# Softmax reciprocals and gates multiplied into the probabilities, and a new entry into each attention stage

## The chip, the cores and the metric

The kernel runs on one core of a Trainium2 chip. The metric is the device time of one execution in microseconds (us), the median of several executions. The engines are named as the profile names them: PE (TensorE matmuls) and PEld (its weight loads), DVE (VectorE), ACT (ScalarE), POOL (GpSimd) and SP (SyncE, which here only issues loads).

## What is computed

Two layers over 256 tokens of 1024 features. Each layer normalises its input, projects it (one weight matrix), runs a dilated attention of 24 heads and a sparse attention of 8 query heads over 2 key heads with three gated branches, merges both, and adds a convolutional FFN. The part that the change touches is the division by the softmax sums:

```
def dilated_mixer(q, k, v):                       # three groups of 8 heads
    for gi, (window, dil) in enumerate(DIL_PAIRS):
        o, lse = banded_attention(...)            # softmax(q k^T / 8) v, and its log-sum
    wts = softmax(stack(lses), axis=0)
    o = sum(wts * stack(outs))
...
    p2 = softmax(s2);  o_sel = p2 @ vg            # selected blocks
    o_win = banded_attention(q, k_win, v_win)     # window
    g = sigmoid(gate_logits)
    o = g[0] * o_cmp + g[1] * o_sel + g[2] * o_win
```

In the dilated attention the three groups of a head share one softmax denominator, so that the result is a sum of unnormalised products divided once.

## The kernel before

**Weights.** All projections stream through `units` of 128 x 2048 fp32, in an order fixed in advance. `load_half` (L208) loads half a unit (512 KB) on SP into one of five `raw` buffers. Each half is split on the chip: ACT casts it to fp32r (`hi`, L238), DVE subtracts (`lo`, L239). A product then takes three matmuls: hi with the activations' high half (L290), hi with their low half (L291), lo with the high half (L292).

**Stages of a layer.** `c10` and `c11` (2 units each: keys and values of the sparse branch, the compressed branch's input), `bq` (its queries), nine chunks of the dilated heads with four `merge` units between, four more merges, two projections, `out`, then the FFN: 22 up units and the down units. The norm's factor 1/rms is worked out beside the first stage: squares are summed into `fin`, summed over partitions by matmuls on `ones` (L344), raised to -1/2 on POOL (L347), copied into the diagonals `dg` (L351), and applied when PSUM is read (L419).

**Attention work.** It is written as generators that run between the weights' matmuls: `tick()`, called after each half chunk, runs one split, the rotary chains (`rope_run`), and one step of up to five active jobs. `job_a(hp)`, four per layer, does two heads' dilated attention, `job_b(hp, t)`, eight per layer, the selected and the window branch of two heads for one block of 128 queries. Both write scores to `pt` (SBUF), take exponentials there with the sums as a by-product, transpose the probabilities on PE (`transposed`, L576), and multiply by the values (`col_pair`, L571). The result lies feature by token, so its division needs the reciprocals along the free axis: DVE copies them, 64 times each, into `drb` (L673, L759), `spread` transposes that with two matmuls (L595), ACT copies the result to `sc` (L597), and DVE multiplies (L706, L772); job_b then adds its two branches (L773).

**Tables and the compressed branch.** POOL multiplies the rotary tables with the gains (`tabs`, L394; `tabc`, L397) once `gr` has landed (L387). `job_cmp1` copies keys (`cdup`, L792), transposes them (L795) and writes them in residue order with copies of a quarter each on ACT (L802).

**Order on the engines.** The scheduler of the tile framework reorders each engine's instructions after that; each engine then runs its list in order, and a wait holds all behind it.

## Time and profile before

| | |
|---|---|
| three timed runs | 965.47, 968.27, 968.22 us |
| median | 968.22 us |
| the profiled execution's own time | 964.59 us |
| its span (first to last instruction) | 962.8 us |
| PE busy | 936.6 us (97%) |
| DVE busy | 753.0 us (78%) |
| ACT busy | 580.2 us (60%) |
| POOL busy | 154.7 us (16%) |
| DMA | 172 GB/s, 165.95 MB |

Busy shares are averages over stages that differ: PE's 97% says that it sets the time nearly everywhere, not that the others have room everywhere. The views of the trace that go further are the list of waits (how long an engine stood idle, and for what), the timeline of a stretch, and busy times by window. In a row, the bracket at the end gives the idle time of the engine ahead of the instruction and what ended it. The granted clock is full in all forty slices of the page.

### The profile page before, as it was taken

The numbers are of one execution on the slowest core, as the hardware profiler recorded it, in microseconds if no ns is written. First come the engines' busy times: TensorE is split into PE (matmuls) and PEld (weight loads), VectorE is DVE, ScalarE is ACT, GpSimd is POOL, SyncE is SP. The second block draws the span as 40 slices with busy tenths as digits, with TensorE's granted clock in tenths as the row PEclk, the third lists the DMA queues.
The fourth block names the chain that finished last, engine by engine and source line by source line (L and its number), as shares of the span: only waits on it lengthen the run. The fifth ranks groups of instructions, "written<-read, shape, count | busy, mean of one in ns | idle before, by whom it ended". The sixth has DMA issues, their size and how long they took to land.

```text
span 962.8 us, 18575 instructions
## 1 busy us (share of the span) xinstructions
PE 936.6 (97%) x7122; PEld 848.9 (88%) x7122; DVE 753.0 (78%) x1595; ACT 580.2 (60%) x1186; POOL 154.7 (16%) x179
## 2 busy tenths in 40 slices
PE   6899999999999999999998999999999999999998
PEld 4778887878999999999986787877799999999998
DVE  6898866887679889986478987678876888998742
ACT  6778665666556555555456986466755555655431
POOL 6140211212002111110122301122200111111000
PEclk9999999999999999999999999999999999999999
DMA  7734446525456565666455344554354465666660
GB/s 242 255 132 155 150 157 207 189 88 174 148 162 213 180 210 187 189 196 204 147 168 174 112 151 135 196 196 140 121 180 153 161 217 175 205 197 203 196 209 19
DMA packets 48041, 165.95 MB, mean 172 GB/s; under 512 B 6096, under 2 KB 7632, under 8 KB 47824
## 3 DMA queue, kind: packets, MB, share of 16 engines
q1 hardware_dynamic: 46800, 163.71, 52.1%
q8 instruction: 56, 0.92, 0.4%
q10 hardware_dynamic: 1152, 1.05, 0.3%
q14 instruction: 33, 0.27, 0.1%
HBM read 163.69 MB, written 1.05 MB: 171 GB/s over the span
## 4 chain that ended last, share of the span: by engine, by line
PE 78%; DVE 10%; ACT 6%; issue 2%; POOL 1%; DMA 1%; SPq 0%; DVEq 0%; ACTq 0%; POOLq 0%
PE acc L373 25%; PE acc L290 5%; PE acc L292 5%; PE acc L291 5%; DVE lo L239 4%; PE acc L1082 4%; PE acc L1084 4%; PE acc L1083 4%; PE acc L957 3%; PE att L571 3%; PE acc L959 3%; PE acc L958 3%; PE att L576 2%; PE acc L993 2%; PE acc L994 2%
## 5 line engine op out<-in xcount | busy, mean ns | idle before, releaser
L239 DVE TENSOR_TENSOR lo<-raw,hi 128x1024 fp32r<-128x1024 f32 (+1 forms) x292 | 368.4, 1279 | 51.6 <-ACT hi L238 49.4
L238 ACT CAST hi<-raw 128x1024 fp32r<-128x1024 f32 (+1 forms) x292 | 294.0, 1037 | 150.9 <-PE acc L291 36.9
L373 PE MATMUL acc<-u,hi 128*128 128x256 f32 x1376 | 236.3, 277 | 0.0
L373 PEld LDWEIGHTS acc<-u,hi 128*128 128x128 f32 x1376 | 207.4, 188 | 0.1
L373 PE MATMUL acc<-u,lo 128*128 128x256 f32 x688 | 190.2, 276 | 0.0
L290 PE MATMUL acc<-hi,hT 128*128 128x512 f32 (+1 forms) x384 | 154.0, 401 | 8.7 <-ACT hi L238 8.7
L292 PE MATMUL acc<-lo,hT 128*128 128x512 f32 (+1 forms) x384 | 150.0, 391 | 5.2 <-DVE lo L239 5.1
L291 PE MATMUL acc<-hi,hT 128*128 128x512 f32 (+1 forms) x384 | 148.5, 387 | 0.0
L373 PEld LDWEIGHTS acc<-u,lo 128*128 128x128 f32 x688 | 129.1, 188 | 0.0
L1084 PE MATMUL acc<-act,lo 128*128 128x256 f32 x352 | 97.2, 276 | 0.0
L1082 PE MATMUL acc<-act,hi 128*128 128x256 f32 x352 | 97.2, 276 | 0.0
L1083 PE MATMUL acc<-act,hi 128*128 128x256 f32 x352 | 97.2, 276 | 0.0
L290 PEld LDWEIGHTS acc<-hi,hT 128*128 128x128 f32 x384 | 72.6, 189 | 25.9 <-ACT hi L238 11.1
L292 PEld LDWEIGHTS acc<-lo,hT 128*128 128x128 f32 x384 | 72.4, 189 | 23.6 <-DVE lo L239 9.2
L291 PEld LDWEIGHTS acc<-hi,hT 128*128 128x128 f32 x384 | 72.7, 189 | 12.6 <-issue 0.3
L957 PE MATMUL acc<-hT,hi 128*128 128x256 f32 x256 | 73.4, 287 | 0.0
L959 PE MATMUL acc<-hT,lo 128*128 128x256 f32 x256 | 71.8, 281 | 0.0
L958 PE MATMUL acc<-hT,hi 128*128 128x256 f32 x256 | 71.7, 280 | 0.0
L1084 PEld LDWEIGHTS acc<-act,lo 128*128 128x128 f32 x352 | 66.1, 188 | 0.0
L1082 PEld LDWEIGHTS acc<-act,hi 128*128 128x128 f32 x352 | 66.1, 188 | 0.0
L1083 PEld LDWEIGHTS acc<-act,hi 128*128 128x128 f32 x352 | 66.1, 188 | 0.0
L1054 POOL TENSOR_TENSOR z<-z,rb 128x512 f32<-128x512 f32 x22 | 30.5, 1386 | 203.1 <-DVE z L1053 203.1
(215 smaller groups left out, 1690.2 us busy)
## 6 DMA issues: line engine op xcount, KB each, us to landing
raw<-in_ws_dram SPq DMA_DIRECT2D x300, 512.0 KB, 4.6
raw<-in_ws_dram SPq DMA_DIRECT2D x8, 280.0 KB, 4.2
x<-in_x_dram SPq DMA_DIRECT2D x1, 1024.0 KB, 9.6
out_dram<-x ACTq DMA_DIRECT2D x8, 128.0 KB, 2.7
gr<-in_g_rope_dram SPq DMA_DIRECT2D x2, 384.0 KB, 4.4
masks<-in_mask_dram SPq DMA_DIRECT2D x1, 576.0 KB, 7.6
xo<-in_xo_dram SPq DMA_DIRECT2D x2, 256.0 KB, 4.5
xo<-in_xo_dram SPq DMA_DIRECT2D x1, 512.0 KB, 7.0
```

Source lines behind the costliest of these rows:

```text
L238: A.copy(h, r)
L239: V.tensor_sub(l, r, h.bitcast(F32))
L290: T.matmul(o, a_hi, b_hi, start=first, stop=False)
L291: T.matmul(o, a_lo, b_hi, start=False, stop=False)
L292: T.matmul(o, a_hi, b_lo, start=False, stop=last)
L373: return [lambda a=a: T.matmul(a[0], a[1], a[2], start=a[3], stop=a[4]) for a in todo]
L957: T.matmul(o, hi[:, k, ms], hT[:, 0, k], start=k == 0, stop=False)
L958: T.matmul(o, hi[:, k, ms], hT[:, 1, k], start=False, stop=False)
L959: T.matmul(o, lo[:, k, ms], hT[:, 0, k], start=False, stop=k == 7)
L1082: T.matmul(ps, hi[:, c], act[:, 0, k], start=k == 0, stop=False)
L1083: T.matmul(ps, hi[:, c], act[:, 1, k], start=False, stop=False)
L1084: T.matmul(ps, lo[:, c], act[:, 0, k], start=False, stop=k == NFT - 1)
```

## The change

It has four parts.

1. **Probabilities scaled.** `job_a` and `job_b` multiply the reciprocals (in `job_b` also the gates) into `pt` by a product per column block, ahead of the transposes; `spread`, `drb`, `sc` and the product on the result go. `job_b`'s two branches accumulate in one PSUM region and leave it with one copy. In `job_a` the reciprocals are four columns per head instead of two, and the yields stand elsewhere; `job_b` normalises the first head one tick after its softmax, and starts with one yield more.
2. **Start.** The first activations and the gain are loaded from ACT's queue, the first unit in quarters on SP; 14 matmuls on `ones` precede the first product; the feeds alternate with the casts; squares are taken in pairs on ACT and added on DVE, none on POOL; c10's first half runs k outside, token block inside.
3. **Entry of each layer.** c10's evictions wait until all of c10 is multiplied; c11 fetches both units and runs token block by token block; `job_cmp1` starts after c11, and its transposes multiply by a permutation, so that the copies `T` are contiguous; the tables are built in three pieces; `dg` is on ACT; the copy `rd` comes a step earlier; `qS` is allocated earlier.
4. **FFN norm.** The norm's matmuls move from before the last weight slice of the first unit to after the third matmul of the second.

```diff
-    A.activation(warm, warm, AF.Square)
+    idle = att()
+    for i in range(14):
+        T.matmul(idle[:, 0:P], ones, ones, start=True, stop=True)
...
+            step = w // 4 if (i, w // 4) in early else w // 2
+            for c0 in range(0, w, step):
...
+        if src is not x:
+            if m % 2:
+                sq = com.tile([P, 2, S], F32, name="sq2", bufs=2)
+                A.activation(sq, src[:, m - 1:m + 1], AF.Square)
+                if m > 1:
+                    V.tensor_add(sq, sq, sums["acc"])
+                sums["acc"] = sq
...
         for t in range(2):
-            V.tensor_scalar(dg[:, t * P:(t + 1) * P], ident, r[:, 1, t:t + 1], None, op0=ALU.mult)
+            A.activation(dg[:, t * P:(t + 1) * P], ident, AF.Copy, scale=r[:, 1, t:t + 1])
...
+            if c == "c11":
+                unit(0)
+                for t in range(2):
+                    for kh in range(2):
+                        if t == 0 and kh == 1:
+                            unit(1)
+                        mms(kh, t, range(4), kh == 0, kh == 1)
+                        if kh == 1:
+                            post_fn(t, ps[t])
+                        tick()
+                return
...
-                        if c == "c10" and t == 0:
+                    if kh == 1 and (c != "c10" or t == 1):
+                        if c == "c10":
                             nrm["col"] = rstd_col()
+                            post_fn(0, ps[0])
                         post_fn(t, ps[t])
...
-        def spread(drb):
-            ps = att()
-            for i in range(2):
-                T.transpose(ps[:, i * P:(i + 1) * P], drb[:, i].rearrange("p a d -> p (a d)"), ident)
-            sc = pool.tile([P, S], F32, name="sc", bufs=1)
-            A.copy(sc, ps[:, 0:S])
-            return sc
...
-            drb = pool.tile([P, 2, 2, 64], F32, name="drb", bufs=1)
-            V.tensor_copy(drb, dr.rearrange("p a t -> p t a")[:, :, :, None].to_broadcast([P, 2, 2, 64]))
+            for a in range(2):
+                for w, (o, n) in enumerate(((0, P), (P, S), (384, S), (640, S))):
+                    V.tensor_scalar(pts[a][:, o:o + n], pts[a][:, o:o + n], dr[:, a, w:w + 1], None, op0=ALU.mult)
+            yield
             yield from take("pT", 2)
             e = [transposed(pts[a], 0, 4) for a in range(2)]
             yield
-            sc = spread(drb)
...
-            V.tensor_tensor(res, o[:, 0:S], sc, op=ALU.mult)
-            split_evac(oT["a"][:, 0, hp], oT["a"][:, 1, hp], res)
+            split_evac(oT["a"][:, 0, hp], oT["a"][:, 1, hp], o[:, 0:S])
...
+            def normalize(a, pt):
+                V.reciprocal(d[:, 1, :, a], d[:, 0, :, a])
+                V.tensor_tensor(d[:, 1, :, a], d[:, 1, :, a], gs[:, t, 1:3, 2 * hp + a], op=ALU.mult)
+                for b in range(2):
+                    V.tensor_scalar(pt[:, b * nk:(b + 1) * nk], pt[:, b * nk:(b + 1) * nk], d[:, 1, b, a:a + 1], None,
+                                    op0=ALU.mult)
...
-            V.tensor_tensor(ob, o[:, 0:S], sc, op=ALU.mult)
-            V.tensor_add(ob_all()[:, hp, tok], ob[:, 0:P], ob[:, P:S])
+            V.tensor_copy(ob_all()[:, hp, tok], o[:, 0:P])
...
-                pg = unit({42: rstd_col}, True)
-                pu = unit({24: lambda: box.update(rb=rstd_row()), 30: lambda: post_g(0, pg)})
+                pg = unit({}, True)
+                pu = unit({3: rstd_col, 27: lambda: box.update(rb=rstd_row()), 33: lambda: post_g(0, pg)})
...
+        A.dma_start(xo[:, 0:2], xv[:, 0:2])
+        A.dma_start(gain, g_norm.rearrange("p (a k) -> p a k", k=8))
+        A.dma_start(xo[:, 2:4], xv[:, 2:4])
...
         for m in range(8):
-            if m in (1, 3):
-                if m == 1:
-                    prepare(0)
+            feed(hT, m, 0, False, xo)
+            if m < 4:
                 pend.popleft()[1]()
-            feed(hT, m, 0, False, xo)
```

How the instructions stand, before and now. Line numbers of the changed kernel are some 4 to 50 higher: L243 is the subtraction `lo`, L242 the cast `hi`, L625 the transposes of the probabilities, L620 the products with the values, L1006 to L1008 a merge's matmuls (before L957 to L959).

PE, layer 0, where the first two products of job_b stand in a merge, before:

```order
L292 MATMUL acc<-lo,hT 128x512
L595 MATMUL att<-ident,drb 128x128 x2
L571 MATMUL att<-pT,vB 64x128 x4
L957 MATMUL acc<-hT,hi 128x256
L958 MATMUL acc<-hT,hi 128x256
L959 MATMUL acc<-hT,lo 128x256
L595 MATMUL att<-ident,drb 128x128 x2
L571 MATMUL att<-pT,vB 64x128 x8
L957 MATMUL acc<-hT,hi 128x256
L576 MATMUL att<-ident,pt 128x128 x2
L958 MATMUL acc<-hT,hi 128x256
```

and the same work now:

```order
L1007 MATMUL acc<-hT,hi 128x256
L625 MATMUL att<-ident,pt 128x128 x4
L1008 MATMUL acc<-hT,lo 128x256
L1006 MATMUL acc<-hT,hi 128x256
L625 MATMUL att<-ident,pt 128x128
L1007 MATMUL acc<-hT,hi 128x256
L625 MATMUL att<-ident,pt 128x128
L1008 MATMUL acc<-hT,lo 128x256
```

and a little later:

```order
L1008 MATMUL acc<-hT,lo 128x256
L1006 MATMUL acc<-hT,hi 128x256
L620 MATMUL att<-pT,vB 64x128 x12
L625 MATMUL att<-ident,pt 128x128 x6
L1007 MATMUL acc<-hT,hi 128x256
```

The two transposes on `drb` ahead of each product are gone, and the transposes of `pt` stand in smaller groups between the merge's matmuls. Over the whole program PE goes from one kind of matmul to another (weights, transposes, attention products) 280 times before and 270 times now, and the transposes by identity or permutation fall from 410 to 362; with the spreads taken out of the order before and all else as it was, the changes of kind would be 252.

DVE, layer 0, behind the reciprocals of job_a for the second head pair, before:

```order
L673 COPY drb<-dr 128x256
L848 TENSOR_TENSOR gl<-gl 128x128
L437 TENSOR_TENSOR t_2111<-qraw,tabs 128x128
L849 TENSOR_SCALAR gl<-gl 128x128
L427 TENSOR_REDUCE rss<-t_2055 128x2
L850 TENSOR_TENSOR gl<-gl 128x128
L377 TENSOR_SCALAR rss<-rss 128x2
L427 TENSOR_REDUCE rss<-t_2059 128x6
L436 TENSOR_TENSOR t_2055<-qraw,tabs 128x128
L377 TENSOR_SCALAR rss<-rss 128x6
L440 TENSOR_TENSOR t_2055<-t_2055,t_2111 128x128
L239 TENSOR_TENSOR lo<-raw,hi 128x1024
```

and now:

```order
L716 TENSOR_SCALAR pt<-pt,dr 128x256
L243 TENSOR_TENSOR lo<-raw,hi 128x1024
L894 SCALAR_TENSOR_TENSOR gl<-gl 128x128
L457 TENSOR_TENSOR t_2045<-t_2045,t_2101 128x128
L896 TENSOR_SCALAR hr<-gl 128x512
L716 TENSOR_SCALAR pt<-pt,dr 128x256 x2
L716 TENSOR_SCALAR pt<-pt,dr 128x128
L716 TENSOR_SCALAR pt<-pt,dr 128x256 x3
L243 TENSOR_TENSOR lo<-raw,hi 128x1024
```

Two of the eight products (one stands seven rows higher) come ahead of the subtraction `lo`, the other six between it and its second half; before, one copy stood there.

ACT at the kernel's start, before:

```order
L310 ACTIVATE hT<-xo,gain 128x256 x2
L238 CAST hi<-raw 128x1024
L310 ACTIVATE hT<-xo,gain 128x256
L325 ACTIVATE sq<-xo 128x256
L310 ACTIVATE hT<-xo,gain 128x256
L325 ACTIVATE sq<-xo 128x256
L310 ACTIVATE hT<-xo,gain 128x256
L325 ACTIVATE sq<-xo 128x256
L310 ACTIVATE hT<-xo,gain 128x256
L325 ACTIVATE sq<-xo 128x256
L238 CAST hi<-raw 128x1024 x2
```

and now:

```order
L314 ACTIVATE hT<-xo,gain 128x256
L242 CAST hi<-raw 128x512
L314 ACTIVATE hT<-xo,gain 128x256
L326 ACTIVATE sq_125<-xo 128x512
L242 CAST hi<-raw 128x512
L314 ACTIVATE hT<-xo,gain 128x256
L242 CAST hi<-raw 128x512
L314 ACTIVATE hT<-xo,gain 128x256
L326 ACTIVATE sq_135<-xo 128x512
L242 CAST hi<-raw 128x512
L314 ACTIVATE hT<-xo,gain 128x256 x2
L326 ACTIVATE sq_144<-xo 128x512
```

Casts of a quarter alternate with the feeds, and squares are taken two slices at a time.

POOL from layer 0's first memset of the job tables on, before:

```order
L784 MEMSET pad 128x16
L806 MEMSET F 128x32 x2
L347 TENSOR_TENSOR rstd<-rstd,mhalf 128x2
L394 TENSOR_TENSOR tabs<-cossin,gr 128x640 x2
L397 TENSOR_TENSOR tabc<-ropec,gr 128x128
```

and now:

```order
L826 MEMSET pad 128x16
L847 MEMSET F 128x32 x2
L411 TENSOR_TENSOR tabs<-cossin,gr 128x2x128 x2
L411 TENSOR_TENSOR tabs<-cossin,gr 128x2x64 x2
L411 TENSOR_TENSOR tabs<-cossin,gr 128x2x128 x2
L359 TENSOR_TENSOR rstd<-rstd,mhalf 128x2
L980 TENSOR_TENSOR tabc<-ropec,gr 128x128
L390 TENSOR_TENSOR rss<-rss,mhalf 128x2 x4
```

All pieces of the tables come ahead of the norm's power; before, the power came first. On SP, `gr` stood ahead of the masks and of three halves of c11, and stands behind them now.

## Rows read from the trace of the kernel before

**Rows 1.** The page, part 1: busy time, share of the span, instructions of each engine
```profile
PE 936.6 (97%) x7122; PEld 848.9 (88%) x7122; DVE 753.0 (78%) x1595; ACT 580.2 (60%) x1186; POOL 154.7 (16%) x179
```

**Rows 2.** Waits of PE, whole span: us in total, times, longest
```profile
PE acc L290 <- ACT hi L238: 8.7, 4, 7.1
PE acc L292 <- DVE lo L239: 5.1, 8, 2.2
```

**Rows 3.** Timeline, first 23 us, ACT and PE: start, us, instruction [idle before <-releaser]
```profile
5.99 1.04 ACT L238 CAST hi<-raw 128x1024 fp32r<-128x1024 f32 x1 [0.67 <-DMA raw<-in_ws_dram]
7.08 0.80 PE L290 MATMUL acc<-hi,hT 128*128 128x512 f32 x1 [7.08 <-ACT hi L238]
15.27 2.54 ACT L238 CAST hi<-raw 128x1024 fp32r<-128x1024 f32 x3
16.35 0.50 PE L290 MATMUL acc<-hi,hT 128*128 128x512 f32 x1 [0.76 <-ACT hi L238]
22.41 0.29 PE L290 MATMUL acc<-hi,hT 128*128 128x280 f32 x1
```

**Rows 4.** Timeline, POOL and DVE around the mixing norms and the first FFN norm
```profile
19.95 3.11 POOL L394 TENSOR_TENSOR tabs<-cossin,gr 128x640 f32<-128x640 f32 x2
21.46 2.10 DVE L351 TENSOR_SCALAR dg<-ident,rstd 128x128 f32<-128x128 f32 x2
310.79 0.48 DVE L351 TENSOR_SCALAR dg<-ident,rstd 128x128 f32<-128x128 f32 x2
489.03 3.42 DVE L337 TENSOR_TENSOR fin<-acc,sq 128x128 f32<-128x128 f32 x2
```

**Rows 5.** Timeline, PE, stalls after c10: layer 0 first and last, layer 1 likewise
```profile
25.77 0.40 PE L292 MATMUL acc<-lo,hT 128*128 128x280 f32 x1 [2.18 <-DVE lo L239]
49.78 0.44 PE L485 MATMUL att<-ident,rd 128*128 128x128 f32 x2 [0.78 <-DVE rd L482]
499.50 0.66 PE L795 MATMUL att<-ident,cdup 128*128 128x128 f32 x4 [1.52 <-DVE cdup L792]
514.89 0.44 PE L485 MATMUL att<-ident,rd 128*128 128x128 f32 x2 [1.81 <-DVE rd L482]
```

**Rows 6.** Timeline, DVE and PE at layer 0's FFN norm
```profile
307.88 0.48 DVE L311 SCALAR_TENSOR_TENSOR u<-x,gain,u 128x256 fp32r<-128x256 f32 x1
308.75 0.61 PE L344 MATMUL att<-ones,fin 128*128 128x1 f32 x4 [1.55 <-DVE fin L333]
```

**Rows 7.** Timeline, PE, one spread in its place
```profile
76.07 0.39 PE L291 MATMUL acc<-hi,hT 128*128 128x512 f32 x1
76.30 0.39 PE L292 MATMUL acc<-lo,hT 128*128 128x512 f32 x1
76.53 0.38 PE L595 MATMUL att<-ident,drb 128*128 128x128 f32 x2
76.84 0.66 PE L571 MATMUL att<-pT,vB 128*64 128x128 f32 x8
```

**Rows 8.** Single lines, DVE: ns min/median/max, first and last start, forms
```profile
L673 DVE COPY drb<-dr x8: 286/290/294, 126.7 to 732.8; 128x256 f32<-128x256 f32 x8
L759 DVE COPY drb<-db x16: 276/287/295, 73.5 to 594.9; 128x256 f32<-128x256 f32 x16
L706 DVE TENSOR_TENSOR res<-att,sc x8: 411/420/424, 142.9 to 743.7; 128x256 f32<-128x256 f32 x8
L849 DVE TENSOR_SCALAR gl<-gl x2: 217/218/220, 174.1 to 648.7; 128x128 f32<-128x128 f32 x2
L855 DVE TENSOR_SCALAR hr<-gl x2: 412/414/415, 178.1 to 652.7; 128x512 f32<-128x512 f32 x2
```

**Rows 9.** Windows: us, busy PE, PEld, DVE, ACT, POOL (instructions), PEclk, DMA, GB/s
```profile
50.00:75.00 25.00, 25.00 (x127) 19.76 (x125) 24.31 (x76) 19.42 (x54) 9.07 (x9) 1.00 0.40 133
530.00:565.00 35.00, 34.87 (x222) 28.31 (x220) 33.50 (x124) 31.65 (x93) 8.47 (x10) 1.00 0.39 130
```

**Rows 10.** Timeline, PE, behind job_a of layer 0's second head pair
```profile
176.92 0.50 PE L292 MATMUL acc<-lo,hT 128*128 128x512 f32 x1 [0.36 <-DVE lo L239]
```

More of the change, by code (lines that the diff above doesn't have):

```diff
@@ L233, in prepare @@
                 else:
-                    raw = load_half(i, c0, w // 2)
-                c = slice(c0, c0 + w // 2)
+                    raw = load_half(i, c0, step)
+                c = slice(c0, c0 + step)
                 def halve(h=hi[:, c], l=lo[:, c], r=raw):
@@ L318, in feed @@
                 V.scalar_tensor_tensor(lo, v, gc, hi.bitcast(F32), op0=ALU.mult, op1=ALU.subtract)
+        if src is not x:
[5 more added lines that the diff above has]
+                sums["acc"] = sq
+            if m == 7:
+                sums["fin"] = com.tile([P, S], F32, name="fin", bufs=1)
+                V.tensor_add(sums["fin"], sq[:, 0], sq[:, 1])
+            return
         if m == 0:
@@ L420, in attention_layer, with rope_run @@
         ready = {"b": 0, "o": 0, "t": 0, 0: 0, 1: 0, 2: 0, 3: 0}
-        def rope_run(raw, kind, t, nh, ksc, fin):
+        def rope_run(raw, kind, t, nh, ksc, fin, pre=None):
             t1 = pool.tile([P, 8, 64], F32, name="t1", bufs=4)[:, :nh]
@@ L489, in fin @@
                 ready["b"] += 1
-            start(rope_run(kraw[:, t, b].rearrange("p (h d) -> p h d", d=64), 3 + b, t, 2, None, fin))
+            start(rope_run(kraw[:, t, b].rearrange("p (h d) -> p h d", d=64), 3 + b, t, 2, None, fin, pre))
         def post_bq(t, ps):
@@ L606, in job_a @@
             ds = pool.tile([P, 2, 4], F32, name="ds", bufs=2)
-            dr = pool.tile([P, 2, 2], F32, name="dr", bufs=2)
+            dr = pool.tile([P, 2, 4], F32, name="dr", bufs=2)
             rows = [slice(0, 64), slice(64, P)]
@@ L750, in job_b @@
             yield
+            normalize(0, p0)
+            p1 = softmax(1, s1)
+            yield
             yield from take("pT", 2)
             e.append(transposed(p0, 0, 2 * (t + 1)))
-            p1 = softmax(1, s1)
+            normalize(1, p1)
             yield
-            yield
-            V.reciprocal(d[:, 1], d[:, 0])
-            V.tensor_tensor(d[:, 1], d[:, 1], gs[:, t, 1:3, 2 * hp:2 * hp + 2], op=ALU.mult)
-            drb = pool.tile([P, 2, 2, 64], F32, name="drb", bufs=1)
-            V.tensor_copy(drb, d[:, 1, :, :, None].to_broadcast([P, 2, 2, 64]))
             e.append(transposed(p1, 0, 2 * (t + 1)))
@@ L762, in job_b @@
             yield
-            sc = spread(drb)
             o = att()
-            for b in range(2):
-                col_pair(o, [(lambda z, b=b: z[:, b * P:(b + 1) * P],
-                              lambda h, b=b, kt=kt: vB[:, kt, b, kv * 64:(kv + 1) * 64],
-                              [e[h][:, b * (t + 1) + kt] for h in range(2)]) for kt in range(t + 1)], True, True)
+            col_pair(o, [(lambda z: z[:, 0:P], lambda h, b=b, kt=kt: vB[:, kt, b, kv * 64:(kv + 1) * 64],
+                          [e[h][:, b * (t + 1) + kt] for h in range(2)]) for b in range(2) for kt in range(t + 1)], True, True)
             give("pT", 2)
             yield
-            ob = pool.tile([P, S], F32, name="res", bufs=1)
-            V.tensor_tensor(ob, o[:, 0:S], sc, op=ALU.mult)
-            V.tensor_add(ob_all()[:, hp, tok], ob[:, 0:P], ob[:, P:S])
+            V.tensor_copy(ob_all()[:, hp, tok], o[:, 0:P])
             ready["o"] += 1
@@ L932, in job_cmp2, with job_tables @@
                 ready["t"] += 1
+        def job_tables():
+            table(2, 3)
+            yield
+            table(0, 2)
+            yield
+            G.tensor_tensor(tabc, ropec, gr[:, :, 5, :], op=ALU.mult)
         chunk_in("c10", 512, post_c10)
+        side.append(job_tables())
+        chunk_in("c11", 280, post_c11)
         side.append(job_cmp1())
-        chunk_in("c11", 280, post_c11)
         nrm["row"] = rstd_row()
@@ L1095, in block_kernel, with quarters @@
         xv = xo_in.rearrange("p (k q) -> p k q", k=8)
-        nc.sync.dma_start(xo[:, 0:2], xv[:, 0:2])
-        nc.sync.dma_start(gain, g_norm.rearrange("p (a k) -> p a k", k=8))
-        early[0, 0] = load_half(0, 0, UW // 2)
+        def quarters(i, h):
+            raw = com.tile([P, UW // 2], F32, name="raw", bufs=5)
+            for j in range(2):
+                c = slice(j * 512, (j + 1) * 512)
+                early[i, h * 1024 + j * 512] = raw[:, c]
+                nc.sync.dma_start(raw[:, c], ws[i][:, h * 1024 + j * 512:h * 1024 + (j + 1) * 512])
+        A.dma_start(xo[:, 0:2], xv[:, 0:2])
+        A.dma_start(gain, g_norm.rearrange("p (a k) -> p a k", k=8))
+        A.dma_start(xo[:, 2:4], xv[:, 2:4])
+        A.activation(warm, warm, AF.Square)
+        quarters(0, 0)
         mhalf = com.tile([P, 16], F32, name="mhalf")
         G.memset(mhalf, -0.5)
-        nc.sync.dma_start(xo[:, 2:4], xv[:, 2:4])
-        early[0, UW // 2] = load_half(0, UW // 2, UW // 2)
+        quarters(0, 1)
         nc.sync.dma_start(xo[:, 4:8], xv[:, 4:8])
```

80 lines of the change are left out of this document (48 added, 32 removed).

## The prediction

> **What bounds the kernel now.** I read the page first: TensorE (PE) is busy 936.6 of 962.8 us [rows 1], so the end is set by how many matmuls there are, at what pace, and by the few places where PE stands still. The view of waits says which these are: the largest two, 8.7 us on ScalarE's (ACT) casts `hi` and 5.1 us on VectorE's (DVE) subtractions `lo`, are waits for a weight half that isn't split yet [rows 2]. The timeline then shows where: nearly all of it lies in the first 17 us [rows 3], where both layers enter their attention stage [rows 5], and at the FFN's norm [rows 6]. Between these PE runs at its pace, 0.23 us from one 128x512 matmul to the next [rows 7]. What the change can win is therefore entry stalls and matmuls taken out; what it can lose is time where DVE, which it loads more, has no slack. DVE is the engine to look at: 24.31 of 25 us busy in 50 to 75 us, and 33.50 of 35 in the same stretch of layer 1 [rows 9].
>
> **The change, part by part.**
>
> *1. Kernel start.* Before, ACT casts the first 512 KB half at 5.99 us and PE starts at 7.08; ACT then works through all eight feeds and their squares before it casts the second unit at 15.27, so PE waits until 16.35, and the first 48 matmuls (c10) end at 22.41 [rows 3]: 15.33 us for what takes 48 x 0.23 = 11.0 at the pace of [rows 7]. Now the first half comes in quarters, from a queue that carries no `xo`, the first cast is half as long, and no square stands on GpSimd (POOL), whose sums ACT's squares waited for. The first cast, at about half of 1.04 us and behind one feed, can end near 6.2 instead of 7.03; the second unit's cast, no longer behind the chain of POOL sums, near 13.2 instead of 16.3. Then 24 matmuls (5.5 us) and about a microsecond for a late `lo` give an end of c10 near 19.9: gain 2.5 us. The 14 idle matmuls on `ones` run while PE would wait for data; if they hang over, they cost at most 0.8 us, and I put them at nothing because the first cast covers them.
>
> *2. Rest of layer 0's entry.* Five more stalls between 22.4 and 50 us add up to 4.46 us: 2.18, 0.37, 0.40, 0.73 and 0.78 (the first and the last of them in [rows 5]). The first is a `lo` that came late because DVE was held: the two `dg` products took 2.10 us together while POOL ran the tables, and 0.48 at the FFN's norm where POOL was idle [rows 4]. Now `dg` is on ACT, `cdup`'s transposes stand inside bq with work ahead of them, c11's units are fetched in one go, and the copies `T` are two instead of eight per head pair, which frees ACT for casts. I leave 1.5 us of the 4.46: gain 3.0. Parts 1 and 2 together 5.5; bounds 2.5 (only the start) and 8 (no stall left).
>
> *3. Layer 1's entry.* Four stalls, 1.52, 0.41, 0.72 and 1.81, again 4.46 us (the first and the last of them in [rows 5]). Same cures; the last is a chain for `rd`, whose copy now comes a step earlier. I leave 1.2: gain 3.3, bounds 1.5 and 4.5.
>
> *4. FFN norm.* PE waits 1.55 us for `fin` at 308.75, and once more in layer 1. Moving the norm's matmuls into the second unit doesn't give that back: the matmuls that are now first need `u`'s low half, which DVE ends at 307.88 + 0.48 = 308.36, only 0.39 earlier [rows 6]. Gain 2 x 0.35 = 0.7, bounds 0 and 1.4.
>
> *5. No spread.* Each of 24 spreads is two transposes that take 0.31 us up to the next matmul [rows 7]; 0.22 of it are the transposes and about 0.09 is the change from one kind of matmul to another, which stays, since the fp32 product follows anyway. 20 x 0.21, and 4 at 0.37 that stood between two groups of fp32 products and go whole: 5.7 us, bounds 4.8 and 7.4 (with every switch). It comes straight off the bound engine. ACT's 24 copies `sc` go too, off the path.
>
> *6. Transposes in smaller groups.* The new order breaks the transposes of the probabilities into more pieces: by the counts, changes of kind fall only from 280 to 270, where taking the spreads out alone would make 252. 18 x 0.09 = 1.6 us lost on PE; bounds 0.8 and 3.
>
> *7. More work on DVE.* The trace has no product by a column on a 128x256 tile. Its neighbours are 218 ns for 128x128 and 414 for 128x512 [rows 8]; on the line through both it is 285 ns. job_a: two heads x (218 + 3 x 285) = 2.15 us, plus two small adds of some 0.16, less `drb` 0.29 and `res` 0.42 [rows 8]: +1.75, x 8 = 14. job_b: four products (0.87 or 1.14), one more reciprocal and one more small product (0.33), the copy out of PSUM about 0.28, less `drb` 0.29, `res` 0.42 and the add about 0.29: +0.48 or +0.75, x 8 each = 10. Together DVE gets 24 us more. Most is hidden: a `lo` half is usually done 3 to 9 us before its first matmul, and from 95 us on DVE has gaps. It isn't hidden in two kinds of place. In 50 to 95 us DVE has under 2 us left [rows 9], and about half of a layer's job_b work (2.5 us) falls there: I take 1 per layer. And behind job_a of the second and third head pair a `lo` is needed at once already (PE waited for one at 176.92 [rows 10]); the new order puts two products ahead of that `lo` and six ahead of its second half, 2.15 us with the adds' 0.3; I take 1 us at each, 2 per layer. Sum 6 us; bounds 2 (only the late `lo`) and 14.
>
> [...] Row: the two 128x128 sums `fin` of layer 1 took 1.71 us each while POOL ran the tables, where a copy of twice that size takes 0.29 [rows 8], and `dg` took four times its later time [rows 4]. [...]
>
> *Sum.* Gains 5.5 + 3.3 + 0.7 + 5.7 = 15.2; losses 1.6 + 6 = 7.6; net 7.6 us off. The profiled execution took 964.59 us (its span 962.8), which gives 957.0. The three timed runs are 965.47, 968.22 and 968.27; the four together average 966.6, which is 2.0 above the profiled one and 1.6 below the median. I take the net off that mean: **959.0 us**, against a median of 968.22 (-1.0%).
>
> **The rivals**, on the same scale.
>
> *A. DVE's additions stay hidden.* Then only the 1.6 and about 1 us are lost, net 12.6: 954.0. For: outside the two saturated stretches `lo` has microseconds in hand. Against: [rows 10], and 24.31 of 25 us.
>
> *B. DVE takes the gain.* The bound of 14 us on the path: gains 15.2 less 15.6, 967.0, within what can't be told from no change. For: in the saturated stretches every product pushes the next `lo`, and a late `lo` holds its raw buffer and the next load. Against: that is over half of the 24.
>
> *C. Layer 0's entry gives nothing.* In the new order POOL runs all tables before the norm's power, where before the power came first, and the tables wait for `gr`, which now stands behind the masks on the load queue. If `gr` lands later than c10's end, the evictions of c10, and with them bq's PSUM tiles, are late: the 5.5 go, net 2.1: 964.5. For: the masks' and `gr`'s transfers compete with weights. Against: c11 lies between and needs neither.
>
> *D. Slower: the new products queue behind POOL.* Place: job_a and job_b in 50 to 135 us and its twin. Price: POOL is busy 9.07 of 25 us there [rows 9]; each of 128 products met with that chance, and lengthened as `dg` was (1.05 instead of 0.24 us each [rows 4]), costs 128 x 0.36 x 0.81 = 37 us on DVE beside the 24. With half of the 61 on the path: 966.6 - 15.2 + 1.6 + 30 = 983. It decides from 13.6 us on the path (less than a quarter of 61), where all gain is gone. [...]
>
> *E. FFN norms give their whole 2 x 1.55:* 2.4 us better than forecast, inside its range.
>
> **How the numbers follow.** A measurement of this kernel can tell about 0.3% (2.9 us) from no change, so faster means below 965.3. Forecast (952 to 964 with the bounds of the terms): 0.58. A, at or below 954: 0.14. C: 0.12, a third of it in the band of no change. B: 0.09. D: 0.07. Faster 0.58 + 0.14 + 0.08 = 0.80; same 0.13; slower 0.07. The range leaves out D and the far ends of A and B: 949 to 968.
>
> **What would show it.** Right: no L595-like transposes and 362 instead of 410 on `ident` or the permutation; first real matmul near 6.2 and c10's end near 20; four entry stalls of layer 1 below 1.5 us in sum; the norm's wait in the FFN replaced by one of about 1.2 us for `u`; DVE near 777 us busy with products of 218 and 285 ns; new or longer PE waits for `lo` just behind job_a of the second and third head pair, 2 us per layer. Wrong: products of half a microsecond and more beside POOL work (D); `rstd` behind the tables with PE waiting for c10's evictions (C); PE waiting for transposes' `pt` or for `lo` by more than 10 us over 50 to 240 us (B); no such wait at all (A).

## The result, and the profile after

The changed kernel takes **955.98 us** (median of four executions, 955.75 to 956.27) against 967.83 (965.47 to 968.27): a ratio of 0.9885, interval 0.987 to 0.990, 11.9 us less. The forecast was 959.0, range 949 to 968. Between the two profiled executions the difference is smaller, 964.59 to 956.27 us, spans 962.8 to 954.5: 8.3 us, against 7.6 in the sum. Two things are therefore to be explained: where the 8.3 come from, and why the medians differ by 3.5 more.

The start times of single matmuls split the 8.3 (before from its timeline, of which [rows 3] shows the first two). The stalls that terms 2 and 3 of the prediction count reach into bq, to the ones at 49.78 and 514.89 in [rows 5]; so two products of bq just behind these are in the table:

| matmul | before | after | difference | gained since the line above |
|---|---|---|---|---|
| first of c10, layer 0 | 7.08 | 7.94 | +0.86 | -0.86 |
| first of c11, layer 0 | 22.41 | 21.36 | -1.05 | 1.91 |
| first of bq, layer 0 | 32.70 | 30.97 | -1.73 | 0.68 |
| 61st product of bq, layer 0 | 49.97 | 46.47 | -3.50 | 1.77 |
| first of c10, layer 1 | 484.83 | 480.37 | -4.46 | 0.96 |
| first of bq, layer 1 | 505.30 | 498.47 | -6.83 | 2.37 |
| 25th product of bq, layer 1 | 515.09 | 506.31 | -8.78 | 1.95 |
| end | 962.8 | 954.5 | -8.3 | -0.47 |

The two added products, before and after, and then two matmuls of job_b's scores after, one in each layer:

```profile
49.97 0.48 PE L290 MATMUL acc<-hi,hT 128*128 128x512 f32 x1
515.09 0.48 PE L290 MATMUL acc<-hi,hT 128*128 128x512 f32 x1
...
46.47 0.39 PE L294 MATMUL acc<-hi,hT 128*128 128x512 f32 x1
506.31 0.47 PE L294 MATMUL acc<-hi,hT 128*128 128x512 f32 x1
...
57.66 0.97 PE L770 MATMUL att<-kS,qS 128*128 128x512 f32 x4 [1.43 <-DVE qS L300]
526.59 0.96 PE L770 MATMUL att<-kS,qS 128*128 128x512 f32 x4 [1.52 <-DVE qS L300]
```

So layer 0's entry brought 3.5 us, where terms 1 and 2 had 5.5, and layer 1's brought 4.3, where term 3 had 3.3. All that comes behind the two entries, for which the sum had a loss of 1.2 (0.7 + 5.7 - 7.6), brought 0.5, although it holds the two new waits for `qS`, 2.95 us. PE's waits after (the view of [rows 2]: total, times, longest):

```profile
PE acc L296 <- DVE lo L243: 4.9, 6, 1.9
PE att L770 <- DVE qS L300: 3.0, 2, 1.5
PE acc L294 <- ACT hi L242: 2.7, 2, 1.9
PE acc L385 <- DVE u L315: 1.2, 2, 0.8
PE acc L1008 <- DVE lo L243: 1.1, 2, 0.6
PE att L625 <- DVE pt L716: 1.1, 2, 0.5
```

L294 and L296 answer to L290 and L292 of [rows 2]: the waits on `hi` shrank from 8.7 to 2.7, mostly because the wait ahead of the very first matmul is now split with the idle matmuls; those on `lo` stayed. The norm's wait on `fin` in the FFN became one on `u`, as the prediction said. The waits on `qS`, ahead of the second group of job_b's first scores (the group at 55.84 doesn't wait, the one at 57.66 does), and on `pt` are new. The busy line, and the new products on DVE (min/median/max ns):

```profile
PE 934.4 (98%) x7102; PEld 851.2 (89%) x7102; DVE 762.1 (80%) x1722; ACT 570.0 (60%) x1164; POOL 151.8 (16%) x177
L716 DVE TENSOR_SCALAR pt<-pt,dr x64: 274/342/352, 122.6 to 727.1; 128x256 f32<-128x256 f32 x48, 128x128 f32<-128x128 f32 x16
L791 DVE TENSOR_SCALAR pt<-pt,db x64: 274/312/351, 67.2 to 582.4; 128x128 f32<-128x128 f32 x32, 128x256 f32<-128x256 f32 x32
```

None of the 128 products took longer than 352 ns, though POOL works beside them: 47 of the 128 ran while POOL had an instruction under way (small powers and copies), 44 of these with POOL first, and job_a's on 128x256 took 342 ns then (median) and 348 otherwise. So nothing in this profile shows the products slowed by POOL's work beside them. DVE is busy 9 us more, not 24: the entry took 7.4 from it (753.0 before, 745.6 in `entry_only` below), and the softmax part added 16.5.

Layer 0's entry in the timeline after, ACT, PE, POOL and DVE:

```profile
6.87 0.51 ACT L314 ACTIVATE hT<-xo,gain 128x256 fp32r<-128x256 f32 x1 [3.21 <-DMA gain<-in_g_norm_dram]
7.94 0.50 PE L294 MATMUL acc<-hi,hT 128*128 128x512 f32 x1 [1.90 <-ACT hi L242]
19.84 3.67 POOL L411 TENSOR_TENSOR tabs<-cossin,gr 128x256 f32<-128x256 f32 x6 [18.13 <-DMA raw<-in_ws_dram]
23.47 0.71 POOL L359 TENSOR_TENSOR rstd<-rstd,mhalf 128x2 f32<-128x2 f32 x1
24.22 0.41 DVE L360 TENSOR_SCALAR rstd<-rstd 128x2 f32<-128x2 f32 x1 [2.52 <-POOL rstd L359]
24.54 0.73 DVE L243 TENSOR_TENSOR lo<-raw,hi 128x560 fp32r<-128x560 f32 x1
25.33 0.39 PE L296 MATMUL acc<-lo,hT 128*128 128x280 f32 x1 [1.92 <-DVE lo L243]
```

Read from the end: PE stands 1.92 us for a `lo`; DVE had stood 2.52 us at the norm's factor, which stands ahead of that `lo` in its list; POOL gave the factor late because six table pieces stood ahead of it, and began those at 19.84, when `gr` was there (issued at 13.63, 6.1 us to landing). That is rival C's chain, and it cost about what `dg` on DVE had cost before (2.18 us, [rows 5]). At the top, ACT's first feed stood 3.21 us for the gain, whose load was issued at 1.17 and landed at 6.78, with the bulk of the others.

### The profile page after: what moved, and what is told of

Its sections match the earlier page's. It is cut to its first block, busy times and chain, and to the rows that moved or that the text cites. A ratio compares the mean times of both kernels' runs of the same rounds, so it can differ in the third digit from the quotient of the medians.

```text
span 954.5 us, 18604 instructions
## 1 busy us (share of the span) xinstructions
PE 934.4 (98%) x7102; PEld 851.2 (89%) x7102; DVE 762.1 (80%) x1722; ACT 570.0 (60%) x1164; POOL 151.8 (16%) x177
## 3 DMA queue, kind: packets, MB, share of 16 engines
HBM read 163.69 MB, written 1.05 MB: 173 GB/s over the span
## 4 chain that ended last, share of the span: by engine, by line
PE 75%; DVE 13%; ACT 6%; DMA 2%; issue 2%; POOL 2%; ACTq 0%; DVEq 0%; POOLq 0%
PE acc L385 26%; PE acc L296 5%; PE acc L294 5%; PE acc L295 5%; DVE lo L243 5%; PE acc L1131 4%; PE acc L1133 4%; PE acc L1132 4%; PE att L620 3%; PE att L625 3%; PE acc L1006 2%; PE acc L1008 2%; PE acc L1007 2%; ACT hi L242 2%; PE acc L1042 2%
## 5 line engine op out<-in xcount | busy, mean ns | idle before, releaser
L243 DVE TENSOR_TENSOR lo<-raw,hi 128x1024 fp32r<-128x1024 f32 (+2 forms) x294 | 369.0, 1271 | 54.5 <-ACT hi L242 52.5
L242 ACT CAST hi<-raw 128x1024 fp32r<-128x1024 f32 (+2 forms) x294 | 293.9, 1030 | 163.0 <-PE acc L295 52.8
L294 PE MATMUL acc<-hi,hT 128*128 128x512 f32 (+1 forms) x384 | 152.6, 397 | 2.7 <-ACT hi L242 2.7
L296 PE MATMUL acc<-lo,hT 128*128 128x512 f32 (+1 forms) x384 | 149.0, 389 | 4.9 <-DVE lo L243 4.9
L296 PEld LDWEIGHTS acc<-lo,hT 128*128 128x128 f32 x384 | 72.2, 188 | 21.9 <-DVE lo L243 7.7
L294 PEld LDWEIGHTS acc<-hi,hT 128*128 128x128 f32 x384 | 72.3, 188 | 19.1 <-ACT hi L242 4.4
L1008 PE MATMUL acc<-hT,lo 128*128 128x256 f32 x256 | 71.8, 281 | 1.2 <-DVE lo L243 1.1
L1006 PE MATMUL acc<-hT,hi 128*128 128x256 f32 x256 | 72.8, 284 | 0.0
```

The lines of the kernel that those rows point to most:

```text
L242: A.copy(h, r)
L243: V.tensor_sub(l, r, h.bitcast(F32))
L294: T.matmul(o, a_hi, b_hi, start=first, stop=False)
L296: T.matmul(o, a_hi, b_lo, start=False, stop=last)
L1006: T.matmul(o, hi[:, k, ms], hT[:, 0, k], start=k == 0, stop=False)
L1008: T.matmul(o, lo[:, k, ms], hT[:, 0, k], start=False, stop=k == 7)
```

## The experiments

Times are medians with the lowest and the highest execution; medians of the kernel before, in the same sessions, lay between 965.8 and 967.4.

**One part alone.** `soft_only` is the kernel before with part 1 of the change; `entry_only` the changed kernel with job_a and job_b as before.

> The kernel before with part 1 alone (scaled probabilities, no spread), entry and norms as before. Theory: the two transposes per spread leave PE for good and the DVE products cost some of it back at places where a lo has no slack: 2 to 5 us faster than before. In the trace: no wait on qS above 1 us before the first scores, since bq ends as late as before; a wait for lo of about 0.6 us behind job_a of the second head pair, one for pt near 0.5 behind the third. Rival (the whole gain is the entry's): within 1 us of before. Rival (DVE takes it): slower by 2 us or more.

> The changed kernel with job_a and job_b as before (spread kept, no scaled probabilities). Theory: the entry is worth 4 to 7 us: c10 ends 1 us earlier in layer 0 and both c11 and bq save 2 us and more in layer 1, but the first scores of job_b then wait for qS, whose lo DVE writes late, so part of what is won at bq's end is given back. Wait on qS stays at 1.4 us per layer if it comes from the entry, and is gone if it comes from the new products. Rival (the softmax carries the gain): under 3 us faster than before.

`soft_only`: 963.97 (962.19 to 966.26), ratio 0.9971, interval 0.9958 to 0.9984. `entry_only`: 959.12 (959.05 to 960.23), 3.1 us above the changed kernel. So the softmax part is worth about 3 us in either surrounding and the entry with the norms the larger part, 5.5 us between the two profiles with an even clock (962.8 and 957.3); the rivals fall. The wait on `qS` is in `entry_only` too (0.73 and 0.49 in layer 0) and nearly gone in `soft_only` (0.4 in all), so it comes with the entry: PE now reaches the scores before DVE and ACT have `qS` ready. The second group of scores, which waits for `qS`, starts 26.7 us behind bq's first one in every kernel with the new entry (27.8 in the two below that load `gr` earlier), wherever bq starts, between 30.6 and 33.6 us. So an earlier bq does bring the scores forward; part of what bq's own later part wins is lost at `qS`.

The spread of `soft_only`'s executions showed something else. Its profile has three stretches in which the granted clock is below full; one, by windows (the columns of [rows 9]), and the matmuls on either side of its beginning:

```profile
305.00:310.00 5.00, 3.53 (x31) 3.33 (x30) 4.25 (x8) 3.36 (x6) 0.79 (x2) 1.00 0.53 161
310.00:315.00 5.00, 5.00 (x30) 4.95 (x29) 2.82 (x5) 2.03 (x3) 0.67 (x1) 0.66 0.83 241
315.00:320.00 5.00, 5.00 (x45) 5.00 (x44) 3.84 (x8) 3.76 (x6) 0.00 (x0) 1.00 0.37 143
...
308.74 0.60 PE L344 MATMUL att<-ones,fin 128*128 128x1 f32 x4 [1.47 <-DVE fin L333]
309.64 0.40 PE L373 MATMUL att<-u,hi 128*128 128x256 f32 x2
311.07 0.63 PE L373 MATMUL acc<-u,hi 128*128 128x256 f32 x2
```

PE stood 1.47 us for the norm, went on at full pace for over a microsecond, and then at little more than half of it (the same pair takes 0.63 instead of 0.40 us, and comes round every 0.64 instead of every 0.35 us). The five microseconds at 0.66 cost 1.7 us (5 x 0.34). The same amount is lost behind two other stalls of this run, about 2 us each, at 24 and at 515 us; its mean granted clock, 0.995 over 963.8 us, makes 4.8 us in all. Each of the three stretches stands behind a stall, though not every stall has one behind it: the clock of the changed kernel is 1.00 from 25 to 30 us, behind its stall of 1.92.

**The norm's place and the clock.** `ffn_old` is the changed kernel with the norm's matmuls where they were, `before_ffn` the kernel before with them moved:

```
-                pg = unit({42: rstd_col}, True)
-                pu = unit({24: lambda: box.update(rb=rstd_row()), 30: lambda: post_g(0, pg)})
+                pg = unit({}, True)
+                pu = unit({3: rstd_col, 27: lambda: box.update(rb=rstd_row()), 33: lambda: post_g(0, pg)})
```

> The changed kernel with the FFN norm's matmuls where they stood before. Theory: PE's gaps there go back from 1.20 and 0.62 to about 1.7 each, 1.5 us slower with an even clock; and a gap of that length lets the granted clock fall for some microseconds in some executions (seen at 309 us of another run: 0.94 over 30 us, 1.8 us lost), so that the executions spread over 3 us again, as those of the kernel before do, and the median is 2 to 4 us above the changed kernel's. Rival (no such link): 0.7 us slower with the same small spread.

> The kernel before with only the FFN norm's matmuls moved as in the change. Theory: 1 to 3 us faster at the median, more than the 0.7 that the waits alone give, and the executions spread less; what spread is left comes from the stalls of 1.8 us and more in the entry. Rival: 0.7 us faster or not to be told from before, spread as before.

`ffn_old`: 958.38 (957.80 to 959.17), 2.4 us above the changed kernel. In its profile layer 1's wait is back at 1.41 us, and behind it two windows have a clock of 0.72 and 0.94, together 1.7 us lost:

```profile
775.60 0.61 PE L356 MATMUL att<-ones,fin 128*128 128x1 f32 x4 [1.41 <-DVE fin L345]
775.00:780.00 5.00, 4.40 (x27) 4.40 (x28) 2.70 (x6) 2.66 (x5) 0.70 (x1) 0.72 0.60 195
780.00:785.00 5.00, 5.00 (x40) 4.95 (x40) 3.92 (x8) 2.05 (x5) 0.00 (x0) 0.94 0.66 209
```

So the small edit is worth 2.4 us here, where the waits themselves differ by 1.0 (0.81 and 1.41 for `fin` against 0.84 and 0.36 for `u`); a second such stretch of this run lies in its start and cost nothing (c11 starts 13.43 us behind the first matmul, as in the changed kernel).

`before_ffn` didn't show it in the median: 966.54 (965.27 to 968.80) against 967.36, ratio 0.9991, interval 0.9975 to 1.0007. My expectation for that one missed in size. The spread did narrow, to 3.5 us over ten executions, where fourteen of before in the same session spread over 5.9 (964.80 to 970.74). The mean granted clock of an execution says why: it is 0.998 or 1.000 in all ten, and 0.995 or 0.996 in seven of the fourteen. At the full clock nothing is won (966.1 against 965.7). Its waits on `fin` are gone, but waits for `dg` (0.5 in each layer) and `u` (0.9 in all) are new there, and its profile has a stretch at 0.66 from 635 us on, behind a wait of 1.6 us for `qkT`. So the norm's place acts by the clock more than by its waits.

Other stalls have the same in their train: six profiles (`before_ffn` and five below) have such a stretch behind a wait for `qkT` of 1.6 to 1.9 us between 622 and 634 us, and none of the profiles where that wait was 1.1 or less has one there. In the five-microsecond windows the clock is 0.66 from 635 us in `before_ffn`, 0.96 and 0.69 from 620 us in `ja_old`, 0.92 and 0.74 from 620 us in `pow_early`, and 1.00 from 620 to 630 us in the changed kernel, whose wait there was 1.0.

**The products and the transposes, each by itself.** `no_scale` leaves out the 128 products (so the outputs of the attention are not divided); `double_scale` follows each by a second one, by 1.0; `entry_nospread` is `entry_only` without the 48 transposes, its factor copied untransposed.

```
 # no_scale
-                    V.tensor_scalar(pts[a][:, o:o + n], pts[a][:, o:o + n], dr[:, a, w:w + 1], None, op0=ALU.mult)
 # double_scale
+                    V.tensor_scalar(pts[a][:, o:o + n], pts[a][:, o:o + n], ones[:, 0:1], None, op0=ALU.mult)
 # entry_nospread
-                T.transpose(ps[:, i * P:(i + 1) * P], drb[:, i].rearrange("p a d -> p (a d)"), ident)
-            A.copy(sc, ps[:, 0:S])
+            A.copy(sc, drb)
```

> The changed kernel without its 128 products of the reciprocals into pt (so the attention outputs are not divided); sums, reciprocals and all matmuls stay. Measures what those products cost. DVE loses 30.5 us of busy time. Theory of the prediction: 6 us of the added DVE work were on the path, so 4 to 8 us faster than the changed kernel, and the waits of PE for lo and pt behind job_a go. Rival (hidden): within 1.5 us of the changed kernel.

> The changed kernel with each of the 128 products into pt followed by a second one by 1.0: 30 us more work on DVE at the places of the added work. Theory now (taking the products away moved nothing, so DVE's additions lie in its gaps): at most 3 us slower than the changed kernel. Rival (the prediction's term: a quarter of DVE's additions land on PE): 6 to 10 us slower, with new waits for lo and pt.

> The changed kernel's entry with the old job_a and job_b, less the 48 transposes of the spreads (the factor is copied from drb untransposed, so the attention outputs are wrong); all DVE and ACT work stays. Measures what the transposes alone cost PE. Prediction's term: 5.7 us faster than the same kernel with them (959.1), bounds 4.8 and 7.4. Rival (about what the whole softmax part brought, 3.1, so that nothing was lost to smaller groups and DVE): 3 to 4 us.

| kernel | median | lowest to highest | span of the profile | DVE busy |
|---|---|---|---|---|
| entry_only | 959.12 | 959.05 to 960.23 | 957.3 | 745.6 |
| entry_nospread | 953.08 | 950.97 to 956.25 | 949.2 | 745.5 |
| changed kernel | 955.98 | 955.75 to 956.27 | 954.5 | 762.1 |
| no_scale | 957.06 | 955.73 to 958.92 | 956.3 | 737.3 |
| double_scale | 973.00 | 971.18 to 974.83 | 969.4 | 789.7 |

The transposes were worth more than I put: 8.1 us between the two profiles with an even clock (957.3 to 949.2), 6.0 between the medians, against 5.7. With every matmul of a trace counted as a product with the weights, a transpose by identity or permutation, or another, PE changes from one kind to another 335 times in `entry_only` and 295 times in `entry_nospread`: at the 0.09 of the sum, 48 x 0.11 + 40 x 0.09 = 8.9, near the measured end (0.6 of the 8.1 are waits: 13.3 and 12.7 us). I had kept a change for each spread; the order without them needs fewer. By this count the kernel before has 344, the same without its spreads 322, and the changed kernel 322: the 18 changes that term 6 of the prediction charges don't show in it.

Taking the products away brings nothing: its profile has one stretch at the lower clock that cost 1.7 us, without which it would be 954.6, the changed kernel's 954.5, and its two executions at the full clock took 955.73 and 955.98. The waits for `pt` and at merges for `lo` are gone (2.2), but others came (`qkT` 1.7 for 1.0, `es` 0.6, `cs` 0.5), 16.6 us in all for 17.0. Doubling them gives DVE 27.6 us more and costs 17. That is more than either expectation had, the rival's 6 to 10 too: DVE's room is just used up. Windows of 100 to 125 us, changed kernel and `double_scale`:

```profile
100.00:125.00 25.00, 24.91 (x208) 19.78 (x207) 20.95 (x84) 18.00 (x53) 3.12 (x6) 1.00 0.54 171
...
100.00:125.00 25.00, 21.47 (x163) 16.30 (x162) 22.34 (x97) 14.73 (x44) 3.18 (x6) 1.00 0.38 127
```

In the first, PE is never held; in the second it stands 3.5 us, for `pT`, `qraw` and `db`, in the stretch behind the saturated one of [rows 9], where DVE's gaps were to take up what was put off. What separates the changed kernel from `entry_nospread`, 5.3 us between the profiles, is then not the products' time. The two traces put it in what the new steps do to PE's list: 322 changes of kind instead of 295 (2.4 at 0.09), and 17.0 us of waits instead of 12.7. `pt` (1.1), `lo` at merges (1.1) and `qkT` (1.0) are not in `entry_nospread`'s list, and `qS` has less there:

```profile
PE acc L296 <- DVE lo L243: 4.3, 6, 1.9
PE att L774 <- DVE qS L300: 1.7, 3, 0.7
```

This is read from two profiles; no run takes the new steps alone.

**Which job carries it.** `ja_old` is the changed kernel with job_a as before.

> The changed kernel with job_a as before (8 spreads kept), job_b as changed. If each spread taken out counts alike, 16 of 24 are gone and two thirds of the softmax part's 3.1 us stay: 957.0, 1.0 slower than the changed kernel. If job_a's eight products per job cost more than its spread (the prediction: 14 of the 24 us of DVE and the late lo behind the second and third head pair), this is as fast as the changed kernel or faster.

955.81 (954.34 to 956.64): as fast as the changed kernel. All of the softmax part's 3 us come from job_b; job_a's eight products and its longer list cost what its spread cost.

**The start.** `no_idle` leaves out the 14 idle matmuls; `gr_early` loads layer 0's `gr` behind the second unit; `both_early` also loads the gain first; `pow_early` puts a tiny copy that needs the power ahead of four table pieces.

```
 # gr_early (its own buffer, after the second unit's halves)
+        load_gr(gr0, 0)
 # both_early, besides
+        A.dma_start(gain, g_norm.rearrange("p (a k) -> p a k", k=8))
         A.dma_start(xo[:, 0:2], xv[:, 0:2])
-        A.dma_start(gain, g_norm.rearrange("p (a k) -> p a k", k=8))
 # pow_early, in job_tables ahead of table(2, 3)
+            if l == 0:
+                G.tensor_copy(tabs[:, :, 0, 0:3, 0], nrm["col"][:, 1, 0:1, None].to_broadcast([P, 2, 3]))
```

> The changed kernel without the 14 idle matmuls on ones. Prediction's view (they cost and bring nothing, the first cast covers them): within 1 us of the changed kernel. Rival (they warm the array): the first real matmuls then go at half pace, 0.42 instead of 0.23 us apart as in the kernel before; some 12 of them, partly beside waits for data, so 1 to 2 us slower, with c10's first half ending after 14.5 us.

> The changed kernel with layer 0's gr in a buffer of its own, loaded right behind the second unit's halves instead of behind the masks. Theory (rival C of the prediction is real in layer 0): in the changed kernel POOL got gr at 19.84, so the tables held the norm's power until 23.47, DVE's copy of it stood ahead of a lo, and PE waited 1.92 us at 25.33 in c11. With gr at about 14 the power runs at about 21.6; that wait falls under 0.5 us and bq starts near 29.3 instead of 30.97: 1 to 1.9 us faster than the changed kernel. Rival (the weights are late anyway, the loads share one queue): the wait stays and time is the same.

> As gr_early, and the gain is loaded ahead of the first activations on ACT's queue (in the changed kernel ACT stood 3.21 us for it, until 6.87, and the first real matmul came at 7.94). Theory: first matmul near 7.0 and, as gr no longer holds c11, another 0.5 to 0.9 us: 2 to 2.8 us faster than the changed kernel in all. Rival (the first activations or the quarter of weights land no earlier): same as gr_early.

> The changed kernel with one tiny copy on POOL (from the norm's power into the tables' place) that forces four of the six table pieces of layer 0 behind the power. Theory: POOL's queue, not gr itself, holds c11: tables(3,5) end near 21.1 instead of 23.5, the power near 22.3, and PE's wait of 1.92 us in c11 falls under 0.5; bq starts 1 to 1.8 us earlier and the time is 954.2 to 955.2 in executions with an even clock. Rival (bq then waits for the later tables or DVE is behind anyway, as the wait on qS at 57 us says): bq starts earlier, the scores of job_b don't, time within 0.5 us of the changed kernel.

`no_idle`: 956.27 (956.14 to 956.44), the same. Yet the idle matmuls do what they seem to: without them the first real ones go 0.43 us apart up to 13.6 us, and c11 starts at 22.22 instead of 21.36 (0.34 of this is the later first matmul, 8.28 for 7.94). The clock column reads 1.00 in that stretch; only the distance of the matmuls shows the lower pace. At bq nothing is left of it (30.93 and 30.97), since PE then waits 1.02 instead of 1.92 us for the same late `lo`:

```profile
24.17 0.42 DVE L357 TENSOR_SCALAR rstd<-rstd 128x2 f32<-128x2 f32 x1 [1.61 <-POOL rstd L356]
25.29 0.40 PE L293 MATMUL acc<-lo,hT 128*128 128x280 f32 x1 [1.02 <-DVE lo L240]
```

`gr_early` 960.70 (957.25 to 962.60) and `both_early` 958.35 (956.45 to 960.76) were slower: both ideas failed. The tables were done by 20.5, but they now ran beside DVE's feeds and splits, which were longer there: the two copies `perm` took 1.23 instead of 0.42 us, a `lo` 1.49 instead of 1.22. PE stood 2.07 us for that `lo`, and the clock was 0.82 over 15 to 20 us and 0.50 over 20 to 25 (up to 3.4 us lost, 5 x 0.18 and 5 x 0.50); it fell once more at 629 us (1.7). The idea itself worked, since c11 took 6.8 instead of 9.6 us in both; but c10 took 18.0 (16.2 in `both_early`) instead of 13.4. First a row of the changed kernel, then `gr_early`:

```profile
14.75 0.42 DVE L394 COPY perm<-ident 128x128 f32<-128x128 f32 x2
...
15.24 5.30 POOL L419 TENSOR_TENSOR tabs<-cossin,gr 128x256 f32<-128x256 f32 x6
16.23 1.23 DVE L400 COPY perm<-ident 128x128 f32<-128x128 f32 x2
17.33 1.49 DVE L249 TENSOR_TENSOR lo<-raw,hi 128x1024 fp32r<-128x1024 f32 x1
18.88 0.79 PE L302 MATMUL acc<-lo,hT 128*128 128x512 f32 x1 [2.07 <-DVE lo L249]
20.00:25.00 5.00, 5.00 (x13) 3.85 (x12) 3.26 (x4) 0.00 (x0) 0.54 (x1) 0.50 0.56 158
```

So DVE's operations took longer beside POOL's tables here (5.30 us for the six pieces), as `fin` and `dg` had in the kernel before [rows 4]; in the attention stretches of the changed kernel, beside POOL's small powers and copies, none of the 128 products did (352 ns at most). Loading the gain first didn't bring the first matmul forward (8.48): the gain landed at 4.80, but then the first activations, now second on the queue, only at 7.32:

```profile
7.41 0.51 ACT L320 ACTIVATE hT<-xo,gain 128x256 fp32r<-128x256 f32 x1 [3.74 <-DMA xo<-in_xo_dram]
```

`pow_early`: 955.28 (954.50 to 957.93). POOL now waits for DVE's sum, and not the sum for six pieces:

```profile
20.27 1.46 POOL L411 TENSOR_TENSOR tabs<-cossin,gr 128x256 f32<-128x256 f32 x2 [18.56 <-DMA raw<-in_ws_dram]
22.67 0.71 POOL L359 TENSOR_TENSOR rstd<-rstd,mhalf 128x2 f32<-128x2 f32 x1 [0.52 <-DVE rstd L358]
23.41 0.17 DVE L360 TENSOR_SCALAR rstd<-rstd 128x2 f32<-128x2 f32 x1 [0.89 <-POOL rstd L359]
```

c11 takes 8.7 instead of 9.6 us, but its first matmul came at 8.76 instead of 7.94, so bq starts at 30.88, as in the changed kernel (30.97), and job_b's scores 24.87 us after it, in both. So the late first matmul hid what c11 gained, and the profile can't tell theory from rival, which both had bq start earlier. It also has two stretches at the lower level, at 9.8 us (0.68 over 10 to 15 us), which cost nothing (c10 took 13.43), and at 624 us (0.92 and 0.74 over 620 to 630 us: 1.7). The executions of `pow_early` and `ja_old` overlap the changed kernel's, so that neither is shown to be faster. The two together weren't tried.

## Why the prediction held, point by point

The time lay 3 us below the forecast, but the terms did not hold as well as their sum. By the profiles with an even clock, the entries with the FFN norm were counted at 9.5 and brought 5.5 (962.8 to 957.3 in `entry_only`); the softmax part was counted as a loss of 1.9 and brought 2.8 (957.3 to 954.5). Errors of -4.0 and +4.7 nearly cancel, so that 7.6 stands beside 8.3 is luck. That the median fell by 3.5 more has a reason that the sum didn't have either (last point).

- **Start (1): too large.** 2.5 us were counted by c10's end, 1.05 came. The failed step is the first cast "near 6.2": it ended near 7.9. I had taken the gain's load for free on its own queue; it landed at 6.8, among 2 MB of others.
- **Rest of layer 0's entry (2): too large.** 3.0 counted; 0.68 came by bq's start and 2.45 by the last stall counted. The chain tables, power, `lo` replaced the one through `dg`; I had it as a rival of 0.12 and left its price out of the term. What bq won after its start went partly into the new wait on `qS` (1.43 us at 57.66), which no part of the prediction had.
- **Layer 1 (3): right within its bounds, somewhat small.** 3.3 counted, up to 4.5 allowed; 2.4 came by bq's start and 4.3 by the last stall counted, less the same wait on `qS` (1.52).
- **FFN norm (4): right by its new wait, not by its time.** The wait is for `u`, as said, and the waits fell by 1.9 us (3.1 to 1.2), more than the 0.7 counted. Yet at the full clock the stretch around them took 158.3 us as before (158.1); why, isn't shown. What the edit brought came by the clock (2.4 us in `ffn_old`), which the prediction didn't have.
- **Spread (5): too small.** 8.1 (6.0 by medians) instead of 5.7, past the upper bound of 7.4.
- **Smaller groups and DVE (6, 7): wrong in kind.** 1.6 + 6 = 7.6 were counted, 5.3 is what separates the profiles, but `no_scale` gives the products no part in it, and the 18 changes of kind don't show in the count; the late `lo` behind job_a of the second pair was there (0.60 for 0.36 us), worth a quarter of a microsecond. The size of one product was off too: 345 and 280 ns, not 285 and 218; my neighbours multiplied by a constant of the program, these by a column, as did `dg` of before, whose eight products on 128x128 took 282 ns in the median.
- **Rivals.** By the profiled executions the forecast was 957.0, A 952.0, and 956.3 came; by the median A came nearer. A is right that the products cost nothing, and wrong that only 2.6 is lost (5.3). C's mechanism was real in layer 0 and cost part of a term, not all (c11 took 2.8 us less with `gr` early). D met POOL about as often as it counted (47 of 128, 0.37 against 0.36), and its price was nothing: none of the 128 took more than 352 ns, and the copies `drb` in the same places had been as even [rows 8], though `gr_early` shows longer operations beside POOL at the start (`perm` 1.23 for 0.42 us). B's mechanism needed twice the products.
- **The median.** The sum was set off the mean of four times of before, 966.6. With the 8.3 of the profiles that gives 958.3; 956.0 came. The changed kernel's four executions lie within 0.5 us, those of before within 2.8. The reason is the clock, by the 33 executions of before that all the runs left: with a mean granted clock of 1.000 they took 965.7 us in the mean (7 of them), with 0.998 966.4 (13), with 0.996 967.8 (10), with 0.995 970.0 (3). The changed kernel took 956.0 at 1.000 and at 0.998 alike. So of the 11.9 us, 9.7 are left at the full clock and some 2 are the clock; the 1.4 between 8.3 and 9.7 is that the profiled execution of before (964.6) was shorter than the mean at that clock, and that of the changed kernel (956.3) the longest of its four. Which stalls of before the stretches follow, its own profile doesn't show, since it has none.

## What to carry to other kernels

Where an engine is 97% in one stretch and 80% overall, test its room from both sides: work taken away may show nothing and the same work added may cost all of it. Price a matmul that is removed with the changes of kind around it, by counting them in both orders. And when a start is made earlier, follow the chain to the first thing that doesn't depend on it: here the norm's factor kept its time (24.22 and 24.17, with the first matmul at 7.94 and 8.28). Compare times at the same granted clock, too: here the clock alone made 2 us of a median.

## What was not expected of the hardware

A wait of PE of 1.4 to about 2 us cost about 1.7 us more than its own length in some executions: full pace for about 1.5 us after it (to 310.2 us in `soft_only`, whose norm starts at 308.74, and to 777.1 in `ffn_old`, whose norm starts at 775.60), then a lower clock (0.66 over five microseconds in `soft_only`, 0.72 and 0.94 over ten in `ffn_old`). In `gr_early`'s start the first matmul behind the wait of 2.07 us was slow already: 0.79 us, where the one behind the wait of 1.90 us in the changed kernel took 0.50. It isn't a rule: in the changed kernel's profile waits of 1.92, 1.43 and 1.52 us had nothing behind them (1.00 in the windows there), nor had any of those in the profile of before, up to 2.18 us (its mean granted clock is 1.000). The 14 matmuls on `ones` spared the first real ones the lower pace (0.43 us from one to the next in `no_idle`, 0.23 in the changed kernel): c11 starts 13.42 to 13.44 us behind the first of these in eight kernels with them, and 13.94 in `no_idle`. In four of the ten profiles with them (`double_scale`, `both_early`, `ffn_old`, `pow_early`, first real matmul at 8.31 to 8.76) the clock was still at 0.68 to 0.78 between 10 and 15 us; in `no_scale` (8.46) and `gr_early` (8.73) it was full there. Except in `both_early`, whose c10 differs, that cost nothing that shows (13.42 to 13.43).
